# Attention in a two-block decoder on one core: values stationary, probabilities moving, two heads in one PSUM bank

## The chip, the cores and the metric

The kernel runs on one core of a Trainium2 chip. The metric is the device time of that core in microseconds, for the whole program. Names used below: PE is the tensor engine (a matmul loads a stationary operand, then streams a moving one past it), DVE the vector engine, ACT the scalar engine, POOL GpSimd, SP the engine that issues most DMAs. SBUF is the working memory of 128 partitions, PSUM the memory that PE writes, in banks of 512 float32 columns by 128 partitions.

## The reference

The reference is a stack of two blocks on 512 tokens of width 1024. The first has a feed-forward part, a mixer and another feed-forward part. The second has two layers, each a four-branch mixer followed by a feed-forward part, on 16 meta tokens plus the 512 tokens. The change lies in two of the four branches, A and B, in both layers:

```
# A: window of 128 keys either side, the 16 meta keys, a bias, and a sink that only the denominator has
s = concat([q.k_band*scale + bias, q.k_meta*scale + bias, sink])     # 4 query heads, 2 key/value heads, width 64
p = softmax(s);  y_a = p_band @ v_band + p_meta @ v_meta             # no value behind the sink
# B: all 528 keys, q and k normed and rotated first
p = softmax(q.k*scale);  y_b = p @ v                                 # 4 query heads, 2 key/value heads, width 64
...
merged = sum over the four branches n of gate[n] * (y_n @ w_branch[n])
h = h + merged @ w_out
```

Two query heads 2p and 2p+1 share the key and value head p; below they are a pair. Layer 0 computes 528 queries, layer 1 the last 512.

## The kernel before

One program runs the parts one after the other. All large activations are kept feature-major (128 features in the partitions, tokens along the columns). Weight products are float32 in three rounded products: each weight tile comes in by DMA as `raw`, ACT rounds it to `wh`, DVE forms the rest `wl`, and `mm3` runs xl x wh, xh x wl and xh x wh (lines of the trace with `<-xl,wh` and so on). The products of attention probabilities with values are plain float32; the trace shows each such matmul as two records, so a count of 600 records is 300 matmuls.

`mixer2(l)` builds one four-branch mixer. Ahead of the change's place stand the branch D (`hgrn`, result Y[3]), the projections, and branch C (Y[2]). Then `attention` runs eight units: A heads 0 to 3, then B heads 0 to 3. It is a pipeline of four steps, one unit apart: the unit's operands are made; `att_max` makes scores query-major in PSUM (`pS`) and takes row maxima on DVE; `att_exp` puts the negated maxima as two more rows under Q and makes scores key-major (`pT`), which ACT turns to P by exp (five slabs, the meta keys first; for A a bias is added on DVE first); `att_pv` multiplies P with V.

`att_pv` before works on one head. For each tile of queries (16 meta and four of 128 in layer 0, four of 128 in layer 1) it loads 128 columns of P as stationary operand and streams V, 64 columns and a 65th of ones. So `po` holds queries in partitions, 64 numerators and a denominator in each group of 65 columns. DVE adds the sink's exp for A (`es`), takes a reciprocal `rec` of a few columns, and multiplies into a token-major slab Y (`scaled`, lines L758 and L760 for the reciprocals). When a pair is complete, `to_features` (L244) turns Y by PE transposes `ptr`, one for each tile of queries, and ACT copies the result into `Yf`, the feature-major slab of Y[branch][pair].

Around it, the generator `gates` makes the gate projections of the mixer (`pgz`, 264 or 512 columns a record), and `fill` lets a few of its matmuls run where a step would leave PE idle; what is left is run by `fill(256)` after `attention`. The scheduler of the tile framework sets the final order on each engine. PSUM tiles `po`, `pS`, `pm`, `pT`, `ptr` come from one pool of four banks (`mx`). After `attention`, each result is split into `Yh` and `Yl`, and the branch products `pbr` run in the order D, C, A, B for each of eight row blocks, multiplied by the gates, followed by the output projection.

Of the kernel before, what the change touches and what calls it, by code (L numbers as in the profile page):

```python
# [13 lines left out]
AF = mybir.ActivationFunctionType  # L14
ALU = mybir.AluOpType
# [4 lines left out]
MT = 16  # L20
NC = NT + MT
# [11 lines left out]
ALL = SEQ + [(0, MT)]  # L33
# [171 lines left out]
class Builder:  # L205
# [494 lines left out]
    def att_exp(self, u):  # L700

        its, mxs, m_row = u["its"], u["mxs"], u["m_row"]
        nit = len(its)
        mst = self.small("mst", 2 * nit, F32R, bufs=3).rearrange("p (t x) -> p t x", x=2)
        n0 = min(4, nit)
        for lo, hi, np_ in ((0, n0, 128), (n0, nit, MT)):
            if lo < hi:
                self.act(mst[:np_, lo:hi, 0], mxs[:np_, lo:hi], AF.Copy, scale=-1.0)
                self.stt(mst[:np_, lo:hi, 1], mxs[:np_, lo:hi], -1.0, mst[:np_, lo:hi, 0].bitcast(F32), ALU.mult,
                         ALU.subtract)  # L710
        Q1, K1, Q2, K2 = u["Q1"], u["K1"], u.get("Q2"), u.get("K2")
        QL = Q1 if Q2 is None else Q2
        for part in ((its,) if nit <= 4 else (its[4:] + its[:2], its[2:4])):
            pm = u["psum"]("pm")
            lo, hi = part[0][0], part[-1][0] + part[-1][1]
            for i0, ni in part:
                self.mm(pm[0:2, i0 - lo:i0 - lo + ni], mst[:ni, its.index((i0, ni)), :], self.idr[:ni, :ni])
            self.acopy(QL[m_row:m_row + 2, lo:hi], pm[0:2, :hi - lo])
        Pt = []
        r = u["r_one"]  # L720
        for j0, nj in u["jts"]:
            a, b = u["qcols"](j0)
            p = self.slab(u["tag"], "P")
            for c, w in self.pieces(a, b - a):
                ps = u["psum"]("pT")
                self.mm(ps[:nj, :w], K1[:r, j0:j0 + nj], Q1[:r, c:c + w], True, K2 is None)
                if K2 is not None:
                    self.mm(ps[:nj, :w], K2[:m_row + 2, j0:j0 + nj], Q2[:m_row + 2, c:c + w], False, True)
                z = p[:nj, c:c + w]
                if u.get("biasR") is None:  # L730
                    self.act(z, ps[:nj, :w], AF.Exp)
                else:
                    self.add(z, ps[:nj, :w], u["biasR"](j0, nj, c, c + w))
            if u.get("biasR") is not None:
                self.act(p[:nj, a:b], p[:nj, a:b], AF.Exp)
            Pt.append((p, nj, a, b))
        u["P"] = Pt

    def att_pv(self, u):

        its, Pt = u["its"], u["P"]
        nit = len(its)
        po = u["psum"]("po")
        for t, (i0, ni) in enumerate(its):
            use = [j for j, (p, nj, a, b) in enumerate(Pt) if a <= i0 and i0 + ni <= b]
            for x, j in enumerate(use):
                p, nj, a, b = Pt[j]
                self.mm(po[:ni, t * 65:t * 65 + 65], p[:nj, i0:i0 + ni], u["V"](j), x == 0, x == len(use) - 1)
            self.fill(2 if t % 2 else 1)
        rec = self.small("rec", nit, bufs=3)  # L750
        den = po[:, :nit * 65].rearrange("p (t x) -> p t x", x=65)[:, :, 64]
        extra = u["extra"](u["mxs"]) if "extra" in u else None
        n0 = min(4, nit)
        for lo, hi, n in ((0, n0, 128), (n0, nit, MT)):
            if lo < hi:
                if extra is not None:
                    self.add(rec[:n, lo:hi], den[:n, lo:hi], extra[:n, lo:hi])
                    self.nc.vector.reciprocal(out=rec[:n, lo:hi], in_=rec[:n, lo:hi])  # L758
                else:
                    self.nc.vector.reciprocal(out=rec[:n, lo:hi], in_=den[:n, lo:hi])  # L760
        u["done"](po, rec)

    def attention(self, units):

        n = len(units)
        live = [None] * n
        for i in range(n + 3):
            if i < n:
                live[i] = units[i]()
            if 0 <= i - 1 < n:  # L770
                self.att_max(live[i - 1])
            if 0 <= i - 2 < n:
                self.att_exp(live[i - 2])
            if 0 <= i - 3 < n:
                self.att_pv(live[i - 3])
                live[i - 3] = None

    def scaled(self, out4, outm, po, rec, its):

        num = po[:, :len(its) * 65].rearrange("p (t x) -> p t x", x=65)  # L780
        self.mul(out4, num[:, 0:4, 0:64], rec[:, 0:4].unsqueeze(2).to_broadcast([128, 4, 64]))
        if len(its) > 4:
            self.ts(outm, num[:MT, 4, 0:64], rec[:MT, 4:5], ALU.mult)

    def to_features(self, y4, ym, sink, psum):

# [670 lines left out]
    def mixer2(self, l):  # L1457
        nc = self.nc
        c0 = 0 if l == 0 else MT
# [29 lines left out]


        V = [self.slab("V", "V") for _ in ALL]
        for t, (_, k) in enumerate(ALL):
            nc.gpsimd.memset(V[t][:k, 0:390].rearrange("p (h x) -> p h x", x=65)[:, :, 64], 1.0)
        qkd = [[self.ps_dram.tile([128, NC], F32, name="qkd") for _ in range(3)] for _ in range(3)]

        def values(t, slot):
            self.turnV(t, ALL, lambda i, ps: self.act(
                V[i][:ALL[i][1], 65 * slot:65 * slot + 130].rearrange("p (h x) -> p h x", x=65)[:, :, 0:64],
                ps.rearrange("p (h x) -> p h x", x=64), AF.Copy, scale=rsc[:ALL[i][1], i:i + 1]), self.acc)

        def tile_of(m, scale, blk):
            t = self.slab("sT", "qk")
# [47 lines left out]

        staged(12, first, sums, roped)

        self.open("at", {"T": 2, "qs": 6, "ks": 4, "p": 10, "y": 2, "u": 2})
        bp = self.tc.tile_pool(name="b2", bufs=1, reuse_waits="tile")
        bpool = bp.__enter__()
        btile = lambda tag: bpool.tile([128, 928], F32, tag=tag, name=tag, bufs=2)
        vs = lambda slot: lambda j: V[j][:ALL[j][1], 65 * slot:65 * slot + 65]
        st = {}

        def out_tiles():  # L1560
# [82 lines left out]
        def product(i, got):  # L1643
            h, t = divmod(i, nit)
            p, x = divmod(h, 2)
            T, T4 = got
            u, ni = heads[h], its[t][1]
            y4, ym = u["y"]
            po = self.mx("po")
            V_ = vs(4 + p)  # L1650
            for j in range(5):
                self.mm(po[:ni, :64], T[:, ni * j:ni * j + ni] if j < 4 else T4[:MT, :ni], V_(j)[:, :64], j == 0, j == 4)
                if j in (1, 3):
                    self.fill()
            o = (y4[:, t] if ni == 128 else ym)[:, 64 * x:64 * x + 64]
            self.act(o, po[:ni, :64], AF.Copy, scale=u["rec"][:ni, 2 * t:2 * t + 1])
            if t == nit - 1 and x:
                self.head_norm(y4, ym, 1.0 - lam_init)
                u["fin"]()
# [3 lines left out]
        def plain(h, b):  # L1663
            p, x = divmod(h, 2)
            if x == 0:
                st["K"] = self.stackK(qkd[b][2][64 * p:64 * p + 64, :], SA, ("T", "ks"))
                out_tiles()
            Q1, Q2 = self.stackQ(qkd[b][p][64 * x:64 * x + 64, :], SQ, ("T", "qs"))
            y4, ym = st["y"]
            fin = finish(b, p)  # L1670

            def done(po, rec):
                self.scaled(y4[:, :, 64 * x:64 * x + 64], None if ym is None else ym[:, 64 * x:64 * x + 64], po, rec,
                            its)
                if x:
                    fin()

            return {"Q1": Q1, "Q2": Q2, "K1": st["K"][0], "K2": st["K"][1], "its": its, "jts": ALL, "r_max": 128,
                    "r_one": 128, "m_row": 64, "psum": self.mx, "tag": "p", "done": done}


        def unitA(h):
# [8 lines left out]
            mq = lambda i, k, a, b: bq[:k, a - i + 400:b - i + 400]  # L1691
            fq = lambda i, k, a, b: self.uq[:k, h, (s := 48 - (i - MT) // 8 if i else 64):s + 16]

            def extra(mxs):
                es = self.small("es", len(its), bufs=2)
                self.act(es[:, 0:4], mxs[:, 0:4], AF.Exp, scale=-1.0, bias=sink)
                if l == 0:
                    self.act(es[:MT, 4:5], mxs[:MT, 4:5], AF.Exp, scale=-1.0, bias=sink[:MT])
                return es

            u.update(V=vs(h // 2), late=late, first=sink, extra=extra,
                     keys=lambda i0: [(0, MT, fq), (max(MT, i0 - 128), min(NC, i0 + (256 if i0 else 144)), mq)],
                     qcols=lambda j0: (max(c0, j0 - 128), min(NC, j0 + 256)) if j0 else (c0, NC),
                     biasR=lambda j, k, a, b: u["br"][:k, a - j + 400:b - j + 400] if j else u["ur"][:k, a:b])
# [2 lines left out]

        def unitB(h):
            u = plain(h, 1)
            u.update(V=vs(2 + h // 2), keys=lambda i0: [(0, 264, None), (264, 528, None)], qcols=lambda j0: (c0, NC))  # L1710
            return u

        self.attention([lambda h=h: unitA(h) for h in range(4)] + [lambda h=h: unitB(h) for h in range(4)])
# [126 lines left out]
```

## Time and profile before

| | us |
|---|---|
| median of 3 runs | 3375.02 |
| range of the runs | 3368.74 to 3382.93 |
| the profiled execution's own time | 3379.54 |
| its span in the trace | 3377.7 |
| stretch of `po` in layer 0, A and B | 1715 to 1850 of the span |
| stretch of `po` in layer 1, A and B | 2765 to 2884 of the span |

The page's busy time adds the durations of the instructions; since matmuls are pipelined, durations of neighbours overlap, and the time that a series takes is read from the start of its first to the start of what follows it. [...]

### The profile page before, as it was taken

How to read it: one execution, taken by the hardware profiler on the slowest of the kernel's cores; microseconds unless marked ns; L12 is line 12 of the kernel's file. 1: busy time of each engine (PE TensorE's matmuls, PEld its weight loads, DVE VectorE, ACT ScalarE, POOL GpSimd, SP SyncE). 2: the span in 40 equal slices, each digit the busy share in tenths (PEclk: the TensorE clock that was granted, in tenths of full speed). 3: DMA queues.
4: the chain of work that ended last, by engine and by line, in shares of the span. 5: the costliest groups of instructions: out<-in, count | busy, mean ns of one | idle time of the engine just before them, and what ended most of it. 6: DMA issues, size and time to landing. Idle time of an engine off the chain costs nothing. (4 is left out here: it accounts for less than half of the span.)

```text
span 3377.7 us, 47662 instructions
## 1 busy us (share of the span) xinstructions
PE 3262.8 (97%) x18886; PEld 2770.6 (82%) x18886; DVE 1722.3 (51%) x3632; ACT 1144.0 (34%) x1958; POOL 468.5 (14%) x575
## 2 busy tenths in 40 slices
PE   8999999899999999998999999999999899999998
PEld 6778778877888889888888999999767788788886
DVE  4443378553544445654763744433665474654433
ACT  4222343366322333222642232222222453232221
POOL 1010010412000013322120300000331221400000
PEclk9999989898999999998997999999999898899999
DMA  4333213322323233233332522233223342522322
GB/s 128 104 107 115 87 63 107 99 88 69 94 94 94 94 100 110 77 102 106 108 115 68 157 88 91 93 99 116 88 84 103 117 130 88 162 90 97 93 93 77
DMA packets 121271, 337.26 MB, mean 100 GB/s; under 512 B 28853, under 2 KB 29248, under 8 KB 121048
## 3 DMA queue, kind: packets, MB, share of 16 engines
q1 hardware_dynamic: 87656, 267.95, 24.8%
q0 software_dynamic: 21712, 54.51, 5.2%
q10 hardware_dynamic: 11680, 11.76, 1.1%
q8 instruction: 148, 2.42, 0.3%
q14 instruction: 75, 0.61, 0.1%
HBM read 298.42 MB, written 39.56 MB: 100 GB/s over the span
## 5 line engine op out<-in xcount | busy, mean ns | idle before, releaser
L269 ACT CAST wh<-raw 128x1024 fp32r<-128x1024 f32 (+1 forms) x448 | 463.7, 1035 | 1571.2 <-issue 766.1
L247 DVE TENSOR_TENSOR wl<-raw,wh 128x1024 fp32r<-128x1024 f32 (+1 forms) x448 | 560.9, 1252 | 412.3 <-ACT wh L269 410.3
L241 PE MATMUL pg<-xl,wh 128*128 128x512 f32 (+1 forms) x880 | 283.2, 354 | 12.7 <-DVE xl L259 12.7
L241 PE MATMUL pg<-xh,wh 128*128 128x512 f32 (+1 forms) x880 | 282.1, 353 | 0.0
L241 PE MATMUL pu<-xl,wh 128*128 128x512 f32 (+1 forms) x880 | 281.2, 352 | 0.0
L241 PE MATMUL pd<-hl,wh 128*128 128x512 f32 (+1 forms) x880 | 281.0, 352 | 0.0
L241 PE MATMUL pu<-xh,wh 128*128 128x512 f32 (+1 forms) x880 | 280.9, 352 | 0.0
L241 PE MATMUL pd<-hh,wh 128*128 128x512 f32 (+1 forms) x880 | 280.7, 352 | 0.0
L241 PE MATMUL pg<-xh,wl 128*128 128x512 f32 (+1 forms) x880 | 280.3, 351 | 0.0
L241 PE MATMUL pu<-xh,wl 128*128 128x512 f32 (+1 forms) x880 | 279.7, 350 | 0.0
L241 PE MATMUL pd<-hh,wl 128*128 128x512 f32 (+1 forms) x880 | 278.5, 349 | 0.0
L241 PE MATMUL pgz<-xl,wh 128*128 128x264 f32 (+1 forms) x768 | 238.6, 360 | 0.0
L241 PE MATMUL pgz<-xh,wh 128*128 128x264 f32 (+1 forms) x768 | 217.8, 333 | 0.0
L241 PE MATMUL pgz<-xh,wl 128*128 128x264 f32 (+1 forms) x768 | 217.6, 332 | 0.0
L247 DVE TENSOR_TENSOR fb<-pu,rs 128x512 f32<-128x512 f32 (+1 forms) x110 | 62.6, 586 | 290.3 <-PE pu L241 290.3
L241 PEld LDWEIGHTS pg<-xl,wh 128*128 128x128 f32 x880 | 153.8, 189 | 38.2 <-DVE xl L259 14.9
L241 PEld LDWEIGHTS pu<-xh,wl 128*128 128x128 f32 x880 | 153.8, 188 | 27.3 <-issue 2.6
L241 PEld LDWEIGHTS pg<-xh,wl 128*128 128x128 f32 x880 | 154.4, 189 | 26.3 <-issue 1.7
L241 PEld LDWEIGHTS pg<-xh,wh 128*128 128x128 f32 x880 | 154.8, 189 | 25.2 <-issue 0.9
L241 PEld LDWEIGHTS pu<-xh,wh 128*128 128x128 f32 x880 | 154.1, 188 | 24.8 <-issue 0.9
L241 PEld LDWEIGHTS pd<-hh,wl 128*128 128x128 f32 x880 | 153.8, 188 | 24.9
L241 PEld LDWEIGHTS pd<-hh,wh 128*128 128x128 f32 x880 | 153.5, 188 | 24.3
(487 smaller groups left out, 6448.9 us busy)
## 6 DMA issues: line engine op xcount, KB each, us to landing
raw<-in_win SPq DMA_DIRECT2D x136, 512.0 KB
raw<-in_gu SPq DMA_DIRECT2D x88, 512.0 KB
raw<-in_f1gu SPq DMA_DIRECT2D x44, 512.0 KB
raw<-in_f2gu SPq DMA_DIRECT2D x44, 512.0 KB
raw<-in_dn SPq DMA_DIRECT2D x32, 512.0 KB
raw<-in_wout SPq DMA_DIRECT2D x24, 512.0 KB
gates<-g POOLq DMA_DIRECT2D x32, 264.0 KB, 2.7
gr<-gates SPq DMA_DIRECT2D x32, 264.0 KB
```

The costliest lines, as they stand in the source:

```text
L241: return self.nc.tensor.matmul(out=out, lhsT=lhsT, rhs=rhs, start=start, stop=stop)
L247: return (eng or self.nc.vector).tensor_tensor(out=out, in0=a, in1=b, op=op)
L269: return self.nc.scalar.copy(out=out, in_=in_)
```

## The change

`att_pv` now takes a pair of heads. The stationary operand is V (64 columns, the two heads share it), the moving operand is P of one head, 264 columns a piece in layer 0 and 512 in layer 1, fewer for A's window. Head 0 writes partitions 0 to 63 of a bank and head 1 partitions 64 to 127, in turn, through tiles of 128 rows by 64 columns of the array (32 by 64 for the 16 meta keys). The result is feature-major at once. A second series with the 64 columns of a constant 1 as stationary operand gives the denominator `pd`, the same in 64 partitions. DVE then adds `es` (A), takes the reciprocal of 128 x 264 or 128 x 512, and multiplies into `Yf`.

For A, the sink's exp is needed along the columns: a matmul `pe` of two rows (the maxima under Q2, ones in K2) repeats the maxima over 128 partitions, and ACT takes the exp into half of a slab `es`. For B, POOL adds the four large slabs of P to one, `tot` (three adds of 128 x 528 or 128 x 512 a head), so that `pd` has two parts in place of five. V is packed at 64 columns a head, the ones column and its memsets go, the pool of P slabs has 12 buffers in place of 10, and the meta slab of P comes from another pool. `scaled`, `done` and the transposes of A and B go; branch C keeps its own.

```diff
@@ att_exp
+        if "sink" in u:
+            z = slice(64 * u["x"], 64 * u["x"] + 64)
+            lo = its[-1][0] if nit > 4 else MT
+            for c, w in self.pieces(lo, NC - lo):
+                pe = u["psum"]("pe")
+                self.mm(pe[:, :w], K2[m_row:m_row + 2, MT:MT + 128], Q2[m_row:m_row + 2, c:c + w])
+                self.act(u["es"][z, c:c + w], pe[z, :w], AF.Exp, bias=u["sink"][z])
...
-            p = self.slab(u["tag"], "P")
+            p = self.slab(u["tag"] if j0 else u["tagm"], "P")
...
+            if "sink" not in u and j0 and len(Pt) > 1:
+                t, c = u["tot"], slice(a, b)
+                self.add(t[:, c], (Pt[0][0] if len(Pt) == 2 else t)[:, c], p[:, c], self.nc.gpsimd)
+                u["sum"] = (t, 128, a, b)
@@ att_pv
-        po = u["psum"]("po")
-        for t, (i0, ni) in enumerate(its):
-            use = [j for j, (p, nj, a, b) in enumerate(Pt) if a <= i0 and i0 + ni <= b]
-            for x, j in enumerate(use):
-                p, nj, a, b = Pt[j]
-                self.mm(po[:ni, t * 65:t * 65 + 65], p[:nj, i0:i0 + ni], u["V"](j), x == 0, x == len(use) - 1)
-            self.fill(2 if t % 2 else 1)
...
+        order = [4, 0, 1, 2, 3]
+        half = [slice(64 * x, 64 * x + 64) for x in range(2)]
+        for c, w in self.pieces(c0, c1 - c0):
+            def products(ps, lhs, parts):
+                todo = []
+                for i, j in enumerate(parts):
+                    for x in range(2):
+                        p, nj, a, b = us[x]["P"][j] if j >= 0 else us[x]["sum"]
+                        a, b = max(a, c), min(b, c + w)
+                        if a < b:
+                            todo.append((x, lhs(j, nj), p[:nj, a:b], a - c, b - c))
+                for i, (x, l, p, a, b) in enumerate(todo):
+                    self.mm(ps[half[x], a:b], l, p, i < 2, i >= len(todo) - 2)
+                    if i % 2:
+                        self.fill()
+
+            po = u["psum"]("po")
+            products(po, lambda j, nj: u["V"](j), order)
+            pd = u["psum"]("pd")
+            products(pd, lambda j, nj: self.ones[:nj, :64], [4, -1] if "sum" in u else order)
+            z = slice(c, c + w)
+            if "es" in u:
+                self.add(r[:, z], pd[:, :w], u["es"][:, z])
+                self.nc.vector.reciprocal(out=r[:, z], in_=r[:, z])
+            else:
+                self.nc.vector.reciprocal(out=r[:, z], in_=pd[:, :w])
+            self.mul(u["Y"][:, z], po[:, :w], r[:, z])
```

On PE, at the first pair of A in layer 0, before (result<-moving,stationary operand, and the partitions x columns of the result):

```order
L241 MATMUL pgz<-xh,wh 128x264 x2
L241 MATMUL po<-V,P 128x65 x14
L241 MATMUL po<-V,P 16x65 x2
L241 MATMUL pS<-K_14380,Q_14481 128x16
```

and after:

```order
L241 MATMUL pgz<-xh,wl 128x264
L241 MATMUL po<-P,V 64x264 x4
L241 MATMUL po<-P,V 64x248 x2
L241 MATMUL po<-P,V 64x120 x2
L241 MATMUL pd<-P,ones 64x264 x4
...
L241 MATMUL po<-P,V 64x264 x2
L241 MATMUL po<-P,V 64x8 x2
...
L241 MATMUL pd<-P,ones 64x256 x2
L241 MATMUL pS<-K_14578,Q_14585 128x264 x2
```

One head's 16 matmuls became the two heads' products and denominators, for two pieces of 264 queries, with no `pgz` between them on either side. On PE, at the end of `attention` in layer 1, before:

```order
L241 MATMUL pT<-Q_25410,K_25283 16x512
L241 MATMUL po<-V,P 128x65 x40
L241 MATMUL pgz<-xl,wh 128x512
L241 MATMUL pgz<-xh,wl 128x512
L241 MATMUL pgz<-xh,wh 128x512
L241 MATMUL pgz<-xl,wh 128x512
L244 MATMUL ptr<-ct,Y 128x128 x4
L241 MATMUL pgz<-xh,wl 128x512
```

and after:

```order
L241 MATMUL pT<-Q_25290,K_25142 16x512
L241 MATMUL po<-P,V 64x512 x10
L241 MATMUL pd<-P,ones 64x512 x2
L241 MATMUL pd<-tot,ones 64x512 x2
L241 MATMUL pbr<-Yl,wh 128x512
L241 MATMUL pbr<-Yh,wl 128x512
```

The last gate products have moved ahead of the last pair, and branch products follow it directly. On DVE, at a pair of A, before (layer 0) and after (layer 1):

```order
L247 TENSOR_TENSOR rec<-po,es 128x4
L247 TENSOR_TENSOR rec<-po,es 16x1
L689 ISA pS,mxs<-pS,uq,rc 128x16
L689 ISA mxs 128x1
L758 RECIPROCAL rec<-rec 128x4
```

```order
L247 TENSOR_TENSOR rec<-pd,es 128x512
L686 TENSOR_REDUCE mx_25071<-pS 128x1
L778 RECIPROCAL rec<-rec 128x512
L247 TENSOR_TENSOR wl<-raw,wh 128x1024
L247 TENSOR_TENSOR Yf<-po,rec 128x512
L686 TENSOR_REDUCE mx_25071<-pS 128x1 x4
```

The reciprocal has grown from 4 columns to 512, and row maxima (`mx`) of the next units and a weight rest (`wl`) stand behind it.

## Rows read from the trace of the kernel before

**Rows 1.** Page: busy us of each engine, share of the span, instructions

```profile
PE 3262.8 (97%) x18886; PEld 2770.6 (82%) x18886; DVE 1722.3 (51%) x3632; ACT 1144.0 (34%) x1958; POOL 468.5 (14%) x575
```

**Rows 2.** Groups by line: matmuls, their weight loads; busy us, mean ns of one, idle

```profile
L241 PE MATMUL po<-V,P 128*128 128x65 f32 (+3 forms) x600 | 100.2, 315 | 0.0
L241 PEld LDWEIGHTS po<-V,P 128*128 128x128 f32 (+3 forms) x600 | 87.8, 211 | 13.0 <-issue 1.2 <-ACT P L266 0.9 <-DVE P L247 0.4
```

**Rows 3.** Windows, tile po alone: us, PE, PEld, DVE, ACT busy, PEclk, DMA, GB/s

```profile
1715.00:1850.00 135.00, 53.87 (x328) 46.11 (x328) 6.52 (x32) 0.00 (x0) 0.85 0.26 82
2765.00:2884.00 119.00, 46.35 (x272) 41.70 (x272) 4.61 (x16) 0.00 (x0) 0.84 0.30 97
```

**Rows 4.** Windows, all work: us, PE, PEld, DVE, ACT, POOL busy, PEclk, DMA, GB/s

```profile
1715.00:1860.00 145.00, 139.56 (x904) 124.64 (x905) 68.01 (x248) 52.20 (x138) 20.23 (x24) 0.82 0.29 89
2765.00:2892.00 127.00, 126.08 (x636) 105.00 (x636) 61.84 (x188) 48.06 (x94) 17.28 (x22) 0.84 0.31 100
```

**Rows 5.** Windows, all work, columns as in rows 4: the clock in layer 0

```profile
1761.00:1784.00 23.00, 22.77 (x174) 20.52 (x172) 13.70 (x45) 10.86 (x30) 4.48 (x5) 1.00 0.40 123
1784.00:1791.00 7.00, 7.00 (x32) 6.02 (x32) 2.75 (x9) 2.11 (x3) 1.32 (x2) 0.53 0.32 97
...
1832.00:1859.00 27.00, 23.87 (x109) 21.14 (x109) 4.47 (x15) 1.41 (x3) 2.63 (x2) 0.50 0.23 71
...
1300.00:1400.00 100.00, 100.00 (x771) 85.54 (x770) 58.64 (x96) 25.93 (x47) 36.39 (x47) 1.00 0.25 78
```

**Rows 6.** Timeline of PE, layer 0: one A head, one B head, the last series

```profile
1768.28 4.64 PE L241 MATMUL po<-V,P 128*128 128x65 f32 x32
1772.85 0.64 PE L241 MATMUL pS<-K,Q 128*128 128x264 f32 x3
...
1798.71 6.32 PE L241 MATMUL po<-V,P 128*128 128x65 f32 x50
1804.97 0.64 PE L241 MATMUL pS<-K,Q 128*128 128x264 f32 x3
1829.00 20.15 PE L241 MATMUL po<-V,P 128*128 128x65 f32 x100
```

**Rows 7.** Timeline of PE: half-array float32 pairs in the branch D

```profile
1418.80 1.16 PE L241 MATMUL pA<-QH,KH 64*128 64x128 f32 x16
1419.89 0.22 PE L241 MATMUL pAm<-QH,KH 64*16 64x16 f32 x4
...
1467.20 0.70 PE L241 MATMUL pA<-QH,KH 64*128 64x256 f32 x4
1467.84 0.51 PE L241 MATMUL pgz<-xl,wh 128*128 128x264 f32 x2
```

**Rows 8.** Timeline of PE: the transposes of one pair, layer 0

```profile
1760.19 0.82 PE L244 MATMUL ptr<-ct,Y 128*128 128x128 f32 x4
1760.77 0.90 PE L241 MATMUL pS<-K,Q 128*128 128x264 f32 x3
```

**Rows 9.** Groups by line on DVE: an ordinary operation and two reciprocals

```profile
L247 DVE TENSOR_TENSOR g<-pgz,rs 128x264 f32<-128x264 f32 (+1 forms) x96 | 47.5, 511 | 101.3 <-PE pgz L241 101.2
...
L760 DVE RECIPROCAL rec<-po 128x4 f32<-128x4 f32 (+1 forms) x12 | 1.6, 163 | 61.7 <-PE po L241 61.7
...
L834 DVE RECIPROCAL be<-be 128x32 f32<-128x32 f32 x1 | 0.4, 352 | 0.0
```

**Rows 10.** Groups by line: a POOL add of the size of those for `tot`

```profile
L247 POOL TENSOR_TENSOR mg<-mg,gr 128x528 f32<-128x528 f32 (+1 forms) x48 | 71.8, 1495 | 72.0 <-DVE gr L259 68.8 <-issue 1.3
```

**Rows 11.** Timeline of PE, layer 1: the end of `attention`

```profile
2867.83 15.62 PE L241 MATMUL po<-V,P 128*128 128x65 f32 x80
2883.38 0.79 PE L241 MATMUL pgz<-xl,wh 128*128 128x512 f32 x1
```

**Rows 12.** Timeline, layer 0: the end of `attention`, ACT and DVE

```profile
1851.85 0.63 ACT L269 CAST Yh<-Yf 128x528 fp32r<-128x528 f32 x1
1852.51 0.71 DVE L247 TENSOR_TENSOR Yl<-Yf,Yh 128x528 fp32r<-128x528 f32 x1 [2.50 <-ACT Yh L269]
```

## What the change will do to the time: the prediction

> **What bounds the kernel now.** The page comes first: PE is busy for 97% of the span, DVE for 51%, ACT and POOL for less [rows 1]. So a microsecond taken from PE is a microsecond of the total, as long as PE does not start to wait for somebody else. Then the groups by line: the products that the change replaces are 600 records with 100.2 us of PE, and their weight loads take 87.8 us beside them [rows 2]. The windows of that tile split them into 53.9 us in layer 0 and 46.4 us in layer 1 [rows 3]. The timeline says why they are dear: one head of A takes 1772.85 - 1768.28 = 4.57 us for 32 records, one of B 1804.97 - 1798.71 = 6.26 us for 50, which is 125 to 143 ns for a record that streams only 65 columns [rows 6]. Each record has a new stationary block of 128 columns, and the load sets the pace. Last, the clock: in these stretches it was 0.82 and 0.84 [rows 4], while the branch before, with PE equally busy, had 1.00 [rows 5]. The stretch at 1761 to 1784 has 1.00 and the next, with the end of a `po` series in it, 0.53; the last two series of layer 0 stand at 0.50 [rows 5] and take 20.15 us for 100 records [rows 6], against 12.5 at the pace of 6.26 for 50. What falls at each place follows a `po` series.
>
> **The products.** Removed: 100.2 us [rows 2]. Added: columns to stream, counted in the new order. A pair of A heads in layer 0 streams 896 + 928 = 1,824 columns a head for `po` and as many for `pd`, 3,648; a pair of B heads 5 parts of 528 for `po` and 2 for `pd`, 3,696; in layer 1 both kinds come to 7 x 512 = 3,584 a head. Two pairs of each kind make 2 x (3,648 + 3,696 + 3,584 + 3,584) = 29,024 columns, in each of the two halves of the array. The price is not in the trace for halves by columns. The nearest rows are halves by rows, also plain float32 and also two heads in turn: 16 records of 128 columns (four pairs of matmuls, 512 columns a half) take 1.09 us, and one pair of 256 columns 0.64 us [rows 7]. Two equations: a column costs (1.09 - 0.64) / 256 = 1.76 ns for both halves together, and 0.19 us is the change of the array's shape. If halves by columns run side by side too, the streams take 29,024 x 1.76 = 51 us. If they run in turn, twice that, 102 us. I take the first, since the rows are the same kind of work. The shape changes at each group's start and end and, around the 16 meta keys, inside: 9 a pair in layer 0 and 5 in layer 1, 4 x 9 + 4 x 5 = 56, at 0.2 us 11 us. Together 62, so PE gains 100.2 - 62 = 38 us. Loads: half as many columns as before at the pace of [rows 6] is some 70 ns a record, under the 225 ns that a record of 264 columns streams for, so they lie beside the stream.
>
> [...] No run here has column tiles yet.
>
> **Transposes.** 32 of 128 columns go, four for each of eight pairs: 1760.77 - 1760.19 = 0.58 us a pair [rows 8], 4.6 us. The ACT copies behind them go too, on an engine with room [rows 1].
>
> **The sink's matmuls.** 12 `pe` matmuls, eight of 264 columns and four of 512, 4,160 columns. Three scores of 264 columns take at most 0.64 us [rows 6], so a column at most 0.81 ns, 3.4 us; and each changes the array's shape twice (two rows), 24 x 0.2 = 4.8 us. Together 8 us, between 2 (the shape changes cost nothing) and 8.
>
> **POOL.** 24 adds of 128 x 528 or x 512 at about 1.5 us [rows 10] are 36 us on an engine that is busy for 20 and 17 us of these stretches [rows 4]. The last add of a head ends some 1.5 us after its last exp; `pd` needs it only after five parts of `po`, which take 5 x 264 x 1.76 ns = 2.3 us or more. I take nothing; without that cover it is 1.5 us a pair of B, 6 us.
>
> **The reciprocals.** A reciprocal of 4 columns takes 163 ns and one of 32 columns 352 ns [rows 9]: (352 - 163) / 28 = 6.75 ns a column, so 264 columns take 1.9 us and 512 columns 3.6 us. An ordinary operation of 264 columns takes 0.51 us [rows 9]; that is the lower bound, and 352 / 32 = 11 ns a column, 2.9 and 5.6 us, the upper. Eight and four of them are 30 us of DVE (6 to 46), where DVE was busy 68 and 62 us of the two stretches [rows 4], so there is room. What counts is who stands behind: on DVE the row maxima of the next units and the weight rests `wl`; on PE the next scores `pS`, which need a bank. In layer 0 two pieces hold two banks each, all four of the pool, until the first multiply by the reciprocal. For the six pairs that have other PE work behind them I take 1.3 us each, between nothing (scores already queued) and the reciprocal's own 1.9 or 3.6, 8 us. At the end of layer 0 the step was bare before, and the reciprocal stands where the transposes and copies stood: nothing. At the end of layer 1 gate products stood behind [rows 11]; they have moved ahead, branch products wait, and 3.6 for the reciprocal, 0.5 for the multiply, 0.63 and 0.71 for the two halves of Y [rows 12] make 5.4 us. Sum: 13 us, between 5 and 30.
>
> [...]
>
> **The clock.** Half clock cost 145 x 0.18 + 127 x 0.16 = 46 us in the two stretches [rows 4]. `po` itself had some 21 of it: at full pace its heads would take 4 x (4.57 + 6.26) + 4 x (28 x 0.143 + 40 x 0.125) = 79 us and not 100 (a head in layer 1 has 28 or 40 records). That is in the 100.2 already. About 25 lie in scores and branch products behind a series. The new series stream for most of their time, as the branch at 1.00 does [rows 5], so these drops could go; but waits for DVE come in. I take half, 13 us back; all of it is 25, none is 0, and a loss is a rival.
>
> **The sum.** -100.2 + 62 - 4.6 + 8 + 13 - 13 = -35 us. From the profiled execution's 3379.5 that is 3345; the median lies 4.5 below that execution, so 3340. The bounds: reciprocals at 5 and all of the clock back give -55, 3320; with `pe` at 2 it is 3314. Reciprocals at 30 and no clock back give -5, 3370; streams at their price and one of the two at its end, 3353 to 3357.
>
> **The rivals.** *Side by side, but the clock falls in the new series.* For it: every `po` series of over 4 us had the clock fall in or right behind it [rows 5, 6], and the new groups last 62 / 8 = 7.8 us each, without other work in between. Against it: halves by rows ran in a branch that kept 1.00. Price: no 13 back, and of eight groups the part behind the first 4.5 us at half pace, 8 x 3.3 = 26 us at most, 13 if half of them: -35 + 13 + 13 = -9, 3366.
>
> *The halves run in turn, and the clock holds.* Then the bank that both heads share gives no second stream, and the change does not do what it says. Against it: [rows 7]; for it: those rows write two banks, and here it is one. Streams 102 in place of 51: -35 + 51 = +16 us, 3391, which no measurement of this kernel (about 0.5%, 17 us) would tell from no change.
>
> *The halves run in turn, and half an array is too little work for the clock.* It decides from the point at which a group lasts beyond some 4.5 us: each would last 113 / 8 = 14 us, as the last series of layers 0 and 1, of 20 and 15.6 us, do, and those stood at about half pace [rows 6, 11]. Place: the eight groups and the work behind them. Price: +16, +13 for the clock that does not come back, and 8 x 9.6 = 77 for the rest of each group at half pace if all of them fall, some 20 if a quarter does. Slower: +49, 3424, and up to 3481.
>
> **How the numbers follow.** The forecast, 3340 with its own 3314 to 3357, has 0.66. The clock's fall has 0.13 (of it 0.04 below 3358), the halves in turn with a full clock 0.10 (0.08 within, 0.02 beyond), the halves in turn at half clock 0.11. Faster by over 0.5%, under 3358: 0.65 + 0.04 = 0.69. Within: 0.01 + 0.09 + 0.08 = 0.18. Slower, over 3392: 0.02 + 0.11 = 0.13. The range leaves out the last rival, half of the one before, and a tail below: 3308 to 3386.
>
> **What the profile after would show.** Products: groups `po<-P,V` and `pd` with starts that make a pair of 264 columns 0.46 us; 0.93 would be halves in turn. A group of a pair some 7 us from first start to what follows. Clock: PEclk of the two stretches above 0.84. DVE: reciprocals of 1.9 and 3.6 us, and PE's idle time before `pS` and before the last `pbr` of layer 1, put down to DVE, at 13 us together. No `ptr` for A and B. The prediction is wrong if a pair of columns costs over 2.6 ns, if reciprocals are much over 11 ns a column, or if the two stretches, 272 us before, do not shrink to about 240.

## The result

The changed kernel takes 3333.19 us (median of 4 runs, 3326.49 to 3336.83) against 3374.40 us (4 runs, 3368.74 to 3382.93): 0.9881, with a 95% interval of 0.9861 to 0.9902. That is 41 us less; the forecast was 3340 and 35 us less. The profiled execution has a span of 3334.7 us.

The page of the profile after (busy us, share of the span, instructions; before in [rows 1]):

```profile
PE 3206.7 (96%) x18654; PEld 2695.6 (81%) x18654; DVE 1746.6 (52%) x3602; ACT 1143.2 (34%) x1946; POOL 499.7 (15%) x589
```

Groups by line of the new matmuls (in place of the 100.2 us of [rows 2]) and of the two reciprocals:

```profile
L241 PE MATMUL po<-P,V 128*64 128x264 f32 (+9 forms) x232 | 41.5, 494 | 0.0
L241 PE MATMUL pd<-P,ones 16*64 16x264 f32 (+8 forms) x136 | 20.4, 423 | 0.0
L241 PE MATMUL pd<-tot,ones 128*64 128x264 f32 (+1 forms) x24 | 5.8, 568 | 0.0
...
L780 DVE RECIPROCAL rec<-pd 128x264 f32<-128x264 f32 (+1 forms) x6 | 13.9, 2324 | 34.7 <-PE pd L241 34.7
L778 DVE RECIPROCAL rec<-rec 128x264 f32<-128x264 f32 (+1 forms) x6 | 13.9, 2313 | 0.1
```

To compare stages, two stretches are used below: from the last product of branch C to the first output projection, in layer 0 and in layer 1. They hold `attention` and the branch products behind it. Windows of before, then of after (us; busy PE, PEld, DVE, ACT, POOL; granted clock; DMA share; GB/s):

```profile
1706.60:1908.10 201.50, 189.85 (x1291) 173.06 (x1291) 114.22 (x348) 65.78 (x156) 50.43 (x47) 0.87 0.39 120
2761.70:2937.70 176.00, 174.07 (x836) 141.90 (x836) 104.45 (x235) 61.67 (x111) 50.68 (x45) 0.88 0.41 135
```

```profile
1703.30:1889.20 185.90, 171.89 (x1209) 139.43 (x1209) 128.70 (x328) 66.31 (x148) 66.52 (x59) 0.90 0.42 130
2742.60:2899.70 157.10, 148.47 (x688) 99.66 (x688) 114.09 (x225) 60.76 (x107) 66.76 (x57) 0.99 0.47 151
```

377.5 us became 343.0: 34.5 less. Each stretch splits by its clock. PEclk is the granted clock of TensorE as a share of full speed; its record in the traces of before and after holds 1.00 and 0.50 alone (31 and 22 spells at 0.50), and half clock is the second. The products `pgz` of 264 columns start every 0.12 us at 1.00 (before, from 1773.45) and every 0.22 us at 0.50 (from 1787.10). The time at half clock, halved, is counted as what the clock took (a stretch of T us at mean clock c: T x (1 - c)); the rest is the work at full clock. Before, the clock took 47.5 us and the work 330.0; after, 20.5 and 322.5 (the clock from its record, finer than the two digits above). So of the 34.5 us, 27 are clock and 7.5 are work. Over all executions the same split, span x clock and span x (1 - clock), gives a mean of 3257 and 117 us for the kernel before (13 executions beside the first experiments) and 3242 and 88 for the changed one: 29 us of clock and 15 of work. The split gives the clock somewhat too much: over the 33 executions of the kernel before that are on record beside the experiments, a microsecond more of span x (1 - clock) comes with 0.78 us more of span, so not all that ran at half clock would have taken half the time at full clock. By an estimate from that 0.78, the clock's 27 us are 21 and the work's 7.5 are 13; where the text below gives the clock's part and the work, it gives the plain split. Outside the two stretches the profiled executions lost 73 us to the clock both before and after: what the change did to the clock, it did inside them. Of the 15 us of work, 7 lie in stages that the change does not touch; the experiments on addresses show where.

One group of a pair of A in layer 0 after the change (PE, timeline: start, us, records):

```profile
1745.11 1.88 PE L241 MATMUL po<-P,V 16*64 16x264 f32 x16
1746.92 1.88 PE L241 MATMUL pd<-P,ones 16*64 16x264 f32 x16
1748.73 2.04 PE L241 MATMUL po<-P,V 16*64 16x264 f32 x20
1750.69 2.04 PE L241 MATMUL pd<-P,ones 16*64 16x264 f32 x20
1752.66 0.51 PE L241 MATMUL pS<-K,Q 128*128 128x264 f32 x2
```

The pair takes 7.55 us from first start to what follows, where the two heads took 2 x 4.57 [rows 6] and a set of transposes.

### The profile page after: what moved, and what is told of

The parts are those of the page before. It is cut to its first block, busy times and chain, and to the rows that moved or that the text cites. A ratio compares the mean times of both kernels' runs of the same rounds, so it can differ in the third digit from the quotient of the medians.

```text
span 3334.7 us, 47150 instructions
## 1 busy us (share of the span) xinstructions
PE 3206.7 (96%) x18654; PEld 2695.6 (81%) x18654; DVE 1746.6 (52%) x3602; ACT 1143.2 (34%) x1946; POOL 499.7 (15%) x589
```

## The experiments

All medians stand beside runs of the kernel before on the same chip; the ratio is to those.

**e1: one half after the other.** This tests whether the halves run side by side at all.

```diff
+                todo.sort(key=lambda t: t[0])
+                n2 = len(todo) // 2
                 for i, (x, l, p, a, b) in enumerate(todo):
-                    self.mm(ps[half[x], a:b], l, p, i < 2, i >= len(todo) - 2)
+                    self.mm(ps[half[x], a:b], l, p, i % n2 == 0, i % n2 == n2 - 1)
```

> Edit: inside each series (po, and pd) all matmuls of head 0 come first, then all of head 1, so neighbours in the queue use the same half of the array; nothing else changes. Theory (the halves run side by side, which is where the gain comes from): the 29,024 columns at 1.7 ns cost once more, +49 us, so about 3382 against 3333 for the changed kernel; a pair of 264 columns takes 0.9 us in place of 0.45. If the clock falls in streams that fill only half of the array, up to 30 us more. Rival (the halves never overlapped much; the gain came from the loads, the transposes and the clock): no change, 3333. Rival in between (the queue finds the other half's work only at the border of the two heads): +40.

Measured: 3383.58 us (10 runs), ratio 1.0024 (1.0009 to 1.0039), 50 us more than the changed kernel. The same series as above (PE, timeline):

```profile
1746.32 3.66 PE L241 MATMUL po<-P,V 16*64 16x264 f32 x16
1749.91 3.66 PE L241 MATMUL pd<-P,ones 16*64 16x264 f32 x16
```

and its two stretches (columns as above):

```profile
1704.50:1910.90 206.40, 192.64 (x1208) 148.71 (x1208) 129.00 (x328) 65.33 (x148) 66.50 (x59) 0.96 0.38 117
2767.90:2950.00 182.10, 173.93 (x687) 107.93 (x688) 113.63 (x225) 60.89 (x107) 67.02 (x57) 0.98 0.41 130
```

A series of 896 columns a head takes 3.59 us in place of 1.81. So the halves do run side by side when their matmuls alternate, and not when they queue in blocks; the +50 us are the +49 of the expectation. The clock is the second answer: the two stretches stand at 0.96 and 0.98, and the groups in them, which stream in half of the array for 13 to 15 us, run at full clock in seven of eight cases. The first of them (window, columns as above):

```profile
1746.32:1761.32 15.00, 15.00 (x74) 7.70 (x73) 4.70 (x7) 1.89 (x4) 1.53 (x1) 1.00 0.21 80
```

Two rivals of the prediction fall with this run: that halves in one bank run in turn, and that half an array is too little work for the clock.

**e2: no reciprocal.**

```diff
-                self.nc.vector.reciprocal(out=r[:, z], in_=r[:, z])
...
-                self.nc.vector.reciprocal(out=r[:, z], in_=pd[:, :w])
+                self.vcopy(r[:, z], pd[:, :w])
```

> Edit: the reciprocal is left out (A multiplies by the sum with es, B by a copy of pd), so the result of A and B is not the quotient; matmuls and their order in the program text are the same. Theory (PE waits for the reciprocal at some pairs and at the end of layer 1): 8 to 13 us less, 3320 to 3325; the 28 us of reciprocals go from DVE, and PE's idle time before pS and before the branch products of layer 1 falls from 3 us and 1 to under 1. Rival (other work stands last at these places, the row maxima or the rounding of Y): under 4 us less, 3330 to 3333.

Measured: 3323.88 us, ratio 0.9843 (0.9823 to 0.9864), 9 us less than the changed kernel. The split of all executions puts it in the work: 3233 us in place of 3242, with the clock's part at 90 and 88. So the reciprocals cost 9 us, though 28 us of them run on DVE; the rest was hidden. (B has a copy in place of each reciprocal, A nothing; an addition of `es` to `pd` of the same size takes 0.43 us for 264 columns and 0.69 for 512 after the change.)

**e3: denominator first.** The order of one piece, for A (`one` is pd, `val` is po; the number is the slab of keys, 4 the 16 meta keys) and for B:

```diff
...
-            products(po, lambda j, nj: u["V"](j), order)
...
-            products(pd, lambda j, nj: self.ones[:nj, :64], [4, -1] if "sum" in u else order)
...
+            if "sum" in u:
+                plan = [(val, 4), (one, 4), (val, 0), (val, 1), (one, -1), (val, 2), (val, 3)]
+            else:
+                plan = [(one, 4), (val, 4)] + [(one, j) for j in range(4)] + [(val, j) for j in range(4)]
...
```

> Edit: the parts of the 16 meta keys of po and pd stand side by side at the start of a piece (3 changes of shape a piece in place of 5, 2 fewer a pair of layer 1, 4 fewer a pair of layer 0: 24 fewer); then for A all of pd, then the rest of po; for B two parts of po, pd from tot, and two parts of po. Theory: 24 x 0.16 = 4 us less, and the reciprocal runs beside the rest of po, 1 us a pair and 2 at the end of layer 1, 6 to 8 less; together 10 to 12, so 3321 to 3323. Rival (PE is released by other work, a change of shape is free beside the loads): 3330 to 3333. Rival (B's pd now waits for POOL's last add): 1 to 2 us a pair more at B, four pairs, 3335.

Measured: 3315.80 us, ratio 0.9817 (0.9799 to 0.9834): 17 us less than the changed kernel, more than expected. A pair of A in layer 1, after the change and then here (PE, timeline):

```profile
2779.57 3.38 PE L241 MATMUL po<-P,V 16*64 16x512 f32 x20
2782.87 3.38 PE L241 MATMUL pd<-P,ones 16*64 16x512 f32 x20
2786.18 0.51 PE L241 MATMUL pS<-K,Q 128*128 128x264 f32 x2
```

```profile
2760.84 1.07 PE L241 MATMUL pd<-P,ones 16*64 16x512 f32 x4
2761.75 1.02 PE L241 MATMUL po<-P,V 16*64 16x512 f32 x4
2762.71 2.37 PE L241 MATMUL pd<-P,ones 128*64 128x256 f32 x16
2764.91 2.32 PE L241 MATMUL po<-P,V 128*64 128x256 f32 x16
2767.16 0.64 PE L241 MATMUL pS<-K,Q 128*128 128x264 f32 x3
```

Here the 1,280 columns of the third row take 2.20 us, 1.72 ns a column for both halves together. The group takes 6.32 us against 6.61 after the change, for two changes of shape fewer: 0.15 us each. So the 24 changes are 3.6 us. The executions split into 3237 us of work and 76 of clock, against 3242 and 88: some 5 of the 17 us are work, 12 are clock. Where the clock's 12 lie, e4 below shows. The second pair of B in layer 0 shows the rival of B in small: its `pd` waits 0.59 us for POOL's last add.

```profile
1808.23 0.44 PE L241 MATMUL pd<-tot,ones 128*64 128x264 f32 x1 [0.59 <-POOL tot L247]
```

**e4: pd from five parts.** The change's POOL adds are left out, so that `pd` of B takes all five parts (in `att_exp`, four lines removed; the order `[4, 0, 1, 2, 3]` is then used by itself).

```diff
-            if "sink" not in u and j0 and len(Pt) > 1:
-                t, c = u["tot"], slice(a, b)
-                self.add(t[:, c], (Pt[0][0] if len(Pt) == 2 else t)[:, c], p[:, c], self.nc.gpsimd)
-                u["sum"] = (t, 128, a, b)
```

> Edit: POOL's adds are left out and pd of B has all five parts. It adds 3 x (528 + 512) x 2 pairs = 6,240 columns in each half. Theory (a column costs 1.7 ns for both halves together, POOL's adds were hidden): +10.6 us, 3344, up to 3349 where layer 0 stands at half clock; POOL loses 31 us. Rival (the halves share something and a column costs 3.4 ns): +21, 3354. Rival (POOL's last add was what PE waited for at B's pairs): +10.6 less 1.5 a pair, 3338.

Measured: 3335.62 us, ratio 0.9877 (0.9856 to 0.9899), which cannot be told from the changed kernel. The split tells more: 3255 us of work, 13 more than the changed kernel and near the expected 10.6, and 78 of clock in place of 88. Why the clock's part is smaller is not settled, but the place can be told. In the profile after, the B pairs of layer 0 stand at half clock; in this one they run at full clock, behind the same wait of PE (1.19 us before the first `pm`). After, then e4 (windows, columns as above):

```profile
1799.00:1826.00 27.00, 26.60 (x114) 14.18 (x114) 5.97 (x5) 8.52 (x23) 7.80 (x6) 0.50 0.03 11
```

```profile
1798.00:1826.00 28.00, 25.04 (x191) 13.29 (x190) 9.57 (x9) 5.58 (x18) 0.00 (x0) 1.00 0.11 34
```

This is no accident of one execution. e2 and e5 (below) issue the same matmuls of B in the same order as the changed kernel, and their profiles have the fall at the same place, before and in the first pair of B in layer 0. e2, then e5:

```profile
1793.20:1817.00 23.80, 23.80 (x103) 13.91 (x102) 4.55 (x8) 9.29 (x26) 6.36 (x6) 0.50 0.08 30
1803.20:1847.50 44.30, 41.18 (x172) 21.77 (x171) 13.28 (x16) 9.26 (x24) 9.34 (x8) 0.50 0.14 49
```

In all three it begins 3 to 4.5 us ahead of the first series of B, so the scores before it, and not the new series, stand at its start. e3, with another order of B, does not have it (nor does e8; e10, in the same order as e3, has 10 us of it). In after, e2 and e5 it costs 12 to 22 us by the split, and the clock's part of e3 and e4 is 12 and 10 us smaller than that of the changed kernel. What starts it is open.

**e7: the kernel before, with wider streams.** After e1 to e4 the clock was the larger part of the gain, so the question was what had cost it before. This edit leaves the loads of P as they are and makes each matmul stream more columns of V than it needs; the 35 more are not read.

```diff
-                self.mm(po[:ni, t * 65:t * 65 + 65], p[:nj, i0:i0 + ni], u["V"](j), x == 0, x == len(use) - 1)
+                self.mm(po[:ni, t * 100:t * 100 + 100], p[:nj, i0:i0 + ni], u["V"](j), x == 0, x == len(use) - 1)
...
-        vs = lambda slot: lambda j: V[j][:ALL[j][1], 65 * slot:65 * slot + 65]
+        vs = lambda slot: lambda j: V[j][:ALL[j][1], 65 * slot:65 * slot + 100]
```

> Edit: in the kernel before, each matmul of P and V streams 100 columns of V in place of 65 (the 35 more belong to other heads and are not read); loads, their number and the order stay. Theory 1 (a series whose pace the loads set loses the clock because PE streams for less than half of it; at 100 columns it streams for two thirds): a record still takes 125 to 143 ns at full clock, and the half clock in the two stretches falls from 47 us lost to about 20, so 3350 for a kernel that does more work. Theory 2 (the clock falls for another reason, a series without other work in between, say): lost time stays at 47, and the total stays at 3376 or grows by the longer streams, up to 10 us.

Measured: 3340.93 us, ratio 0.9899 (0.9879 to 0.9919). A kernel that streams half as much again for nothing is 36 us faster, within 8 us of the changed kernel. The products' group, and the two stretches (columns as above):

```profile
L241 PE MATMUL po<-V,P 128*128 128x100 f32 (+3 forms) x600 | 88.6, 286 | 0.0
```

```profile
1701.80:1888.00 186.20, 175.18 (x1292) 157.82 (x1292) 114.92 (x348) 66.06 (x156) 50.77 (x47) 0.98 0.42 130
2740.20:2901.10 160.90, 158.77 (x835) 126.05 (x835) 104.08 (x235) 61.63 (x111) 51.65 (x45) 1.00 0.46 148
```

The clock took 3.4 us of these stretches in place of 47.5. The work at full clock went up, 330.0 to 343.7: one head of A takes 4.92 us (1736.91 - 1731.99, below) in place of 4.57 [rows 6].

```profile
1731.99 4.99 PE L241 MATMUL po<-V,P 128*128 128x100 f32 x32
1736.91 0.51 PE L241 MATMUL pS<-K,Q 128*128 128x16 f32 x3
```

So theory 1 holds in its main point (the short streams behind full loads cost the clock), and its detail that the pace would not change is wrong by 4% to 9%, depending on the kind of head. e7 does not part the longer streams from this slightly slower pace, which comes with them.

**e5 and e6: addresses.** The stages that the change does not touch were not equal before and after. A third of the gate products of the last feed-forward part (512 columns; shortest, median, longest ns, then first and last start) in before and after:

```profile
L241 PE MATMUL pg<-xl,wh x176: 396/397/398, 2988.5 to 3230.7; 128*128 128x512 f32 x176
```

```profile
L241 PE MATMUL pg<-xl,wh x176: 391/394/398, 2949.0 to 3188.9; 128*128 128x512 f32 x176
```

242.2 us became 239.9. The clock is 1.00 throughout this stage in all profiles. The change removes the small tiles `rec` and `es`, and by that all large slabs lie 160 bytes lower in each partition. e5 puts a constant of 160 bytes behind the small tiles of the changed kernel, e6 one of 96 behind those of the kernel before:

```diff
             self.ps_sm = P(name="sm", bufs=1)
+            pad = P(name="pad", bufs=1).tile([128, 40], F32, name="pad")
+            nc.vector.memset(pad, 0.0)
```

> Edit: the changed kernel with a constant of 160 bytes a partition behind the small tiles, so that the large slabs lie at the addresses they had before (the change took small tiles away and so moved them down by 160 bytes). Why: in the changed kernel the feed-forward stages of 512 columns, which the change does not touch, are 1% shorter (362.6 us from 366.0 in the last one, most matmuls 232 ns from start to start in place of 232 to 236). Theory (the address of the moving operand sets that pace): these stages go back to 366, the first two with them, and the whole is 8 us longer, 3341. Rival (another chip or execution): 3333, stages at 362.6.

> Edit: the kernel before with 96 bytes a partition more behind the small tiles, so that its large slabs lie at the changed kernel's addresses modulo 128. Theory of the addresses: the feed-forward stages of 512 columns fall from 366 to 362.6 us, the one of 528 tokens rises from 378 to 380, the whole 3376 to about 3368. Rival: no change, 3376. It is also a second profile of the clock of the kernel before: in the stretches from the end of the branch C to the output projections I expect some 45 us lost to half clock again, as the first profile has 47.

The same row in e5 and in e6:

```profile
L241 PE MATMUL pg<-xl,wh x176: 392/397/398, 2960.7 to 3202.8; 128*128 128x512 f32 x176
```

```profile
L241 PE MATMUL pg<-xl,wh x176: 391/394/397, 2991.0 to 3231.0; 128*128 128x512 f32 x176
```

242.1 and 240.0: the pace follows the shift, both ways. It repeats closely: from the first to the last start of all products of this stage it is 371.4 us in the profiles of before, e5 and e7, and 367.9 to 368.0 in those of after, e1 to e4, e6 and e9. e6 takes 3368.03 us, ratio 0.9975 (0.9957 to 0.9993), as expected; its split is 3250 us of work (before 3257) and an unchanged 117 of clock, and its two stretches lost 53 us to the clock, so the 47 of the first profile was no accident. e5 takes 3334.16 us, ratio 0.9887 (0.9855 to 0.9919), not the 3341 expected, but one of its four runs is at 3351.6 and the interval holds both; its work is 3249 against 3242, so the 7 us are in the split and not in the median.

**e8 and e10: other addresses.** e3 with 64 and with 96 bytes more, by the same edit.

> Edit: the kernel with the denominator first (e3) with 64 bytes a partition more behind the small tiles. Theory (what counts is the address of the moving operand modulo 64, which stays): same as e3, 3316. Rival (modulo 128 or more counts): the stages of 512 columns at 366 and the whole at 3324, or faster still.

> Edit: e3 with 96 bytes a partition more behind the small tiles, which puts the moving operands of 512 columns at 0 modulo 128; 64 is the kernel before (last feed-forward stage 366.0 us), 32 the changed kernel (362.6), 96 was e8 (363.4). The pieces of 264 columns lie at 0 and 32; 64 and 96 gave 378.3 for the feed-forward stage of layer 0, 32 and 64 gave 380.0, 96 and 0 gave 381.7. If alignment to 64 is what is slow, 366 and 381, the whole at 3324; if only 64 is slow, 362 to 363 and 380, 3316.

Measured: e8 3322.39 us (0.9843, 0.9822 to 0.9864), e10 3323.28 us (0.9854, 0.9828 to 0.9879). The row of the gate products, in e8 and in e10:

```profile
L241 PE MATMUL pg<-xl,wh x176: 389/395/401, 2937.6 to 3178.1; 128*128 128x512 f32 x176
L241 PE MATMUL pg<-xl,wh x176: 391/394/403, 2937.1 to 3178.6; 128*128 128x512 f32 x176
```

The part of the last feed-forward stage that runs without interruption takes 363.4 and 365.1 us, against 362.6 in e3 and 366.0 before; the one of layer 0, in pieces of 264 columns, 381.7 and 380.6, against 380.0 and 378.3. So neither of the two simple rules that I had offered (modulo 64; only one bad place) holds. What is shown is a spread of about 1% between addresses 32 bytes apart; the rule behind it stays open.

**e9: the lesson tried elsewhere.** The edit is to e3, in the attention of the first block; of the 96 columns the 64 wanted ones are read.

```diff
...
-                self.mm(po[:, :64], T[:, cs], V[j][:, 64 * h:64 * h + 64], j == 0, j == 3)
+                self.mm(po[:, :96], T[:, cs], V[j][:, 128 * p + 32 * x:128 * p + 32 * x + 96], j == 0, j == 3)
...
```

> Edit: e3 (denominator first), and in the attention of the first block, which the change does not touch, each matmul of P and V streams 96 columns of V in place of 64. There 256 records, four at a time between other work, stand in a stretch at clock 0.90 in which PE is busy for 135 of 152 us (e3). Theory 1 (what cost the clock in A and B, short streams behind full loads, costs it here too): up to 12 of the 15 us lost there come back for about 256 x 20 ns = 5 us more streaming, so 3308 to 3312 against e3's 3316. Rival (four records at a time are no series; here PE's idle time or the changes between kinds of work cost the clock): lost time stays, 3316 to 3321.

Measured: 3312.39 us (3307.33 to 3318.44), ratio 0.9823 (0.9790 to 0.9856). Beside e3 at 3315.80 this is no difference that these runs can tell: the split is 3236 and 75 us, e3's 3237 and 76. The profile says more of the stage itself. From the first to the last of the edited matmuls, e3 and then e9 (windows, columns as above):

```profile
720.50:832.40 111.90, 102.72 (x559) 79.89 (x558) 37.33 (x132) 73.75 (x159) 25.77 (x33) 0.87 0.27 78
722.10:826.40 104.30, 94.63 (x550) 73.74 (x550) 37.60 (x132) 73.34 (x159) 26.82 (x33) 0.93 0.29 84
```

The same stretch takes 110.4 to 113.4 us at 0.85 to 0.88 in all eleven profiles without the edit. So in this profile the clock took 7 us of the stretch in place of 14, and the work at full clock stayed at 97: theory 1 at half its size. It is one execution, and the total does not show it. e3 and e9 are both faster than either kernel of this study.

## Why the prediction was right, step by step

**What bounds the kernel** was read rightly: PE's time and PE's clock.

**The products.** Forecast: 100.2 us removed and 62 added. From start to start the old series took 99.3 us in the trace, the new ones 65.6, of which 9 are the clock; at full clock 79.7 and 56.7. The price from the half-array pairs of [rows 7], 1.76 ns a column and 0.19 us a change of shape, was 1.72 and 0.15 (e3). Halves by columns behave as halves by rows do, in one bank too. Side by side they gain close to two: e1's 3.59 us against 1.81 is a factor of 1.98.

**The clock** is the step whose weight the text had wrong, and its size somewhat too large. I put 21 us of half clock into the removed products and took 13 of the other 25 back, 34 together, with a product gain of 17 at full clock beside it. Measured were 27 in the profiled stretches and 29 over all executions, less by the estimate with 0.78. But the text presented a change that takes work from PE, with a clock that comes back as a by-product. e7 turns this round: with the old loads, the old transposes and more columns, the clock gives 36 us net of 12 to 14 more of work. The cause that I named, a series whose pace the loads set, is borne out by it: behind the same loads the 47.5 us became 3.4.

One reading under the rivals was wrong: that every `po` series of over 4 us had the clock fall in it or right behind it. Three of fourteen had no such fall, those from 1768.28 (4.57 us), 1798.71 (6.26 us) and 2816.04 (4.14 us). From their start to the next series, before (windows, columns as above):

```profile
1768.28:1784.40 16.12, 16.12 (x123) 14.53 (x121) 7.13 (x28) 7.24 (x21) 4.86 (x5) 1.00 0.51 166
1798.71:1813.90 15.19, 14.33 (x113) 12.72 (x112) 9.14 (x25) 6.82 (x21) 0.00 (x0) 1.00 0.16 53
2816.04:2827.60 11.56, 11.56 (x67) 9.59 (x66) 6.89 (x19) 5.30 (x12) 3.67 (x4) 1.00 0.54 181
```

So the 4.5 us from which both rivals of the clock counted half pace rest on no rows, and the new groups do not bear them out: the groups of A after the change, of 6.61 and 7.55 us, and seven groups of 13 to 15 us in e1 ran at 1.00 to their end. The rival in which the clock falls in the new series happened in one place, the B pairs of layer 0, in the three profiles with that order (after, e2, e5); it began ahead of the series, e3 and e4 do not show it, and what starts it is open.

**The reciprocals** were sized at 1.9 and 3.6 us and measured 1.80 and 3.34 (tile `rec` after: shortest, median, longest ns):

```profile
L778 DVE RECIPROCAL rec<-rec x6: 1793/1803/3343, 1749.4 to 2814.4; 128x264 f32<-128x264 f32 x4, 128x512 f32<-128x512 f32 x2
```

13 us of waiting was forecast and e2 gave 9. At the end of layer 1 PE's idle time is 3.1 and 1.4 us, near the 5.4 taken. In layer 0 the wait for a bank is there as described, but small: it is the row of `pS` and `Yf` (waits of PE in the stretch of layer 0, then of layer 1: us in total, times, longest). The first row is no wait that the change made; before it was 8.3 us.

```profile
PE pbr L241 <- DVE mg L259: 8.9, 8, 2.7
PE pS L241 <- DVE Yf L247: 1.8, 2, 1.2
PE pm L241 <- DVE mst L259: 1.2, 1, 1.2
```

```profile
PE pbr L241 <- DVE mg L259: 3.1, 1, 3.1
PE pbr L241 <- DVE Yl L247: 1.4, 1, 1.4
```

From 264 to 512 columns a further column costs (3.34 - 1.80) / 248 = 6.2 ns, where the two reciprocals of [rows 9] gave 6.75.

**The sink's matmuls** came to 0.32 us each for 264 columns and 0.41 for 512, 4 us in all and not 8: I had priced a column by a row that holds a start. One of them, after the change (PE, timeline):

```profile
1742.30 0.38 PE L241 MATMUL pe<-Q,K 2*128 2x264 f32 x1
1742.62 1.72 PE L241 MATMUL pT<-Q,K 128*128 128x272 f32 x10
```

**POOL's adds** took 1.3 us and were hidden, as said. **The transposes** went.

**The sum.** Forecast for the two stretches -35 us, measured -34.5. At full clock the terms would make -23 for the products, about -5 for the transposes, +4 for `pe` and +8 for PE's longer waits, -16; the plain split measures -7.5, the estimate with 0.78 some -13. So most of that difference lies in the split, and 2 to 3 us can't be placed. (e5's stretches hold 319.2 us of work against 322.5, but its profiled execution lost 12 us more to the clock there, and at 0.78 that alone makes 2.6 of the 3.3; no effect of addresses inside the stretches is shown.)

That -35 meets -34.5 so closely is in part luck. The forecast has 34 us of clock and 1 of work; measured are 27 and 7.5, or 21 and 13. The clock was put too high, and the products at full clock (-17 for -23), `pe` (8 for 4) and the waits (13 for 8 to 9) too dear, and the two errors cancel.

**What no step had** is the 160 bytes. They give 7 us in stages outside the change, about the distance between the 35 forecast and the 41 measured.

## What to carry to other kernels

Split a stretch into work at full clock and time taken by the clock before pricing an edit: here more than half of a gain that looked like fewer and denser matmuls was the clock, and a kernel that streams 35 unused columns gained 36 us against the change's 41. Check the split against several executions of one kernel, as the 0.78 does here. Where a series loads 128 columns to stream 65, give each load more columns to stream, or swap the operands, as here. When two heads share the array by halves, let them alternate in the queue (queued in blocks they cost 50 us here, e1), put the product that DVE needs first in front, and keep equal shapes together (0.15 us a change of shape, e3); that order was worth another 17 us, most of them clock.

## What was not expected

A shift of all large slabs by 160 bytes changes the pace of matmuls that nobody edited by 1%: 366.0 us to 362.6 in the last feed-forward stage (512 columns), and the other way, 378.3 to 380.0, for the pieces of 264 columns. The kernel before gains 9 us from 96 unused bytes (e6). A change that adds or removes a small tile can move the total by this much with no cause in its own stage.

The clock's part also differs between executions of one kernel: for the kernel before it ranges from 104 to 132 us over the 13 executions beside e1, while the whole ranges over 22 us. The two go together (0.78 us of the whole for each of the clock's part), so the clock is enough to explain that spread.
